# Forgetting attention with 66-row score matmuls: the cumulative gate sums ride in two more rows of the query and key tiles

## The chip, the cores and the metric

The kernel runs as one program on one core of a Trainium2 chip. The metric is the device time of one execution in microseconds (us), and the times shown are medians of several runs. The core's engines run side by side, each through its own list of instructions, and wait for each other on semaphores: TensorE (PE in the profile; its weight loads are a row of their own, PEld), VectorE (DVE), ScalarE (ACT), GpSimd (POOL) and SyncE (SP), which here issues nearly all DMA transfers.

## The reference

Two layers of a decoder trunk on 512 positions of 1024 channels. Each layer is a half-step SwiGLU feed-forward, a mixer with four gated branches, and a second feed-forward. The branches are a Conformer convolution, a short gated convolution, a sliding-window attention, and the forgetting attention ("fox") that this change touches:

```
def _forgetting_attention(q, k, v, log_f):        # 4 heads of 64
    cum = jnp.cumsum(log_f, axis=1)
    ...
        s = jnp.einsum("bqhd,bkhd->bhqk", q_blk, k, ...) * (dh ** -0.5)
        s = s + (c_blk[..., :, None] - cum_k[:, :, None, :])
        s = jnp.where(kpos[None, :] <= qpos[:, None], s, NEG_INF)
        p = jax.nn.softmax(s, axis=-1)
        return jnp.einsum("bhqk,bkhd->bqhd", p.astype(v.dtype), v)
```

`q` and `k` are RMS-normalised over their 64 channels and scaled by a per-channel weight; `log_f` is the log-sigmoid of a gate plus a bias, one per head and position. So a score is a 64-long dot product plus the query position's cumulative gate sum minus the key position's.

## The kernel before, in words

Activations are kept transposed: channels on the 128 partitions, 512 positions along the row. Every float32 product is made of three fp32r matmuls on a high and a low part of each operand (`mm3`, L227 to L230: high by high, low by high, high by low). ScalarE rounds a tile to its high part and VectorE subtracts to get the low part (`split`, L232). Weights stream in from HBM in 512 KB chunks through the SP queue (`load_one`, L185).

The big projections accumulate in four PSUM banks with the tag `mm`; everything else ("background" work of attention and norms) uses the other four banks, tag `bg`. Background work is written as Python generators. `tick()` (L121) is called between two pieces of projection work and moves each active generator one step on, so that attention matmuls stand between projection matmuls. From what is thus written, a scheduler makes the final order on each engine: an instruction may move past others when its inputs or its buffer are not ready by the scheduler's own reckoning. Buffers named `L0`, `L1`, ... (`LT`, L99) exist once; a new tile under the same name has to wait until all reads of the old one are over.

In the mixer, the projection `F` (group F, L646) makes the fox queries and keys, with positions on the partitions, in four `mm` banks. `qk_norm` (L456) copies them to `L0` to `L3`, computes the norm factors, multiplies, and then, one 128-column tile per tick, transposes them with four 128x128 TensorE transposes (L480) into a `bg` bank and splits that into high and low (L483 on ScalarE, L136 on VectorE). Two heads of 64 share the 128 partitions of one tile, so that there are two query tiles and two key tiles.

`forget` (L490) computes `log_f` and its cumulative sums: a tile `lg` with 32 columns per head, of which four are filled, is multiplied in plain float32 with a triangle of ones (L513, four matmuls of 512, 384, 256 and 128 columns). The result has the sums on partitions 32h to 32h+3 for head h. From it, VectorE makes `bq` and `bk`, four rows per head: high and low part of the sum on one side, ones on the other.

`fox_unit(h, i)` (L527) makes the scores of head h and query block i, 256 to 512 columns wide, in one `bg` bank with five matmuls: high by high with 64 rows (L534), the causal mask as a bf16 matmul with the identity, 128 rows (L535), the two cross terms with 64 rows (L536, L537), and `bq` by `bk` with 4 rows (L538). Softmax follows on VectorE and ScalarE, then a transpose of the probabilities (L554) and the product with the values (L569 to L571). There are 4 heads x 4 blocks = 16 units in a layer. Of the four widths of a head, two are 256, one is 384 and one is 512.

After group F, `branch` (L728) runs 8 output tiles for each of the four branches; for tile d a gate projection (24 matmuls into one `mm` bank), six branch matmuls into another, a tanh on ScalarE (L739) and a multiply on VectorE that frees the second bank. In the first branch that multiply writes its result to `L0` to `L7` (`mg_[d]`), where `L0` to `L3` held the untransposed fox queries and keys.

Of the kernel before, what the change touches and what calls it, by code (L numbers as in the profile page):

```python
# [67 lines left out]
def _trunk(tc, xin, wst, wa, wv, wf, par, relb, cst, out):  # L68
# [66 lines left out]
    def stt(o, i0, s, i1, a, b):  # L135
        return V.scalar_tensor_tensor(out=o, in0=i0, scalar=s, in1=i1, op0=a, op1=b)  # L136
# [13 lines left out]
    ones = ct[:, C_ONE:C_ONE + P]  # L150
    one = ct[:, C_1:C_1 + 1]
    ident = ct[:, C_ID:C_ID + P]
    tri = ct[:, C_TRI:C_TRI + S]

    def cm(i):
        return ct[:, C_M + i:C_M + i + 1]

    def pc(l, o, n=1):
        return pt_[:, l * NPAR + o:l * NPAR + o + n]
# [238 lines left out]
    def mixer(l, st, nxt):  # L398
# [54 lines left out]
                confT.append((hi, lo))  # L453
                yield

        def qk_norm(pv, zs, nq, n, offs, res, done):  # L456


            v = T([P, NB, n], F32, f"v{n}")
            for j in range(NB):  # L460
                sq = TP()
                A.copy(zs[j][:, 0:64 * n], pv[j][:, 0:64 * n])
                A.activation(sq[:, 0:64 * n], pv[j][:, 0:64 * n], AF.Square)
                V.tensor_reduce(v[:, j, :], sq[:, 0:64 * n].rearrange("p (h c) -> p h c", c=64), AX.X, ALU.add)
            ts(v[:, :, 0:nq], v[:, :, 0:nq], 1.0, 64 * EPS, ALU.mult, ALU.add)
            ts(v[:, :, nq:n], v[:, :, nq:n], 1.0 / 64, EPS, ALU.mult, ALU.add)
            r = rsq(v.rearrange("p j h -> p (j h)"), NB * n)
            for j in range(NB):
                z = zs[j][:, 0:64 * n].rearrange("p (h c) -> p h c", c=64)
                rj = r[:, j * n:(j + 1) * n].rearrange("p (h o) -> p h o", o=1).to_broadcast([P, n, 64])  # L470
                V.tensor_mul(z, z, rj)
            yield
            yield
            yield
            yield
            for t in range(n // 2):
                yield
                ps = PSB()
                for j in range(NB):
                    nc.tensor.transpose(ps[:, j * P:(j + 1) * P], zs[j][:, t * P:(t + 1) * P], ident)  # L480
                g = pc(l, offs[t])
                hi, lo = LT(res + 2 * t), LT(res + 2 * t + 1)
                A.activation(hi, ps, AF.Identity, scale=g)  # L483
                stt(lo, ps, g, f(hi), ALU.mult, ALU.subtract)
                done.append((hi, lo))


        bq, bk = T([P, S], F32R, "bq"), T([P, S], F32R, "bk")

        def forget():  # L490
            z = fl.rearrange("p j h -> p (j h)")
            ab, e, w, t = SM(16), SM(16), SM(16), SM(16)
            ts(ab, z, -1.0, None, ALU.mult)
            V.tensor_tensor(out=ab, in0=ab, in1=z, op=ALU.min)
            A.activation(e, ab, AF.Exp)
            ts(w, e, 1.0, None, ALU.add)
            A.activation(t, w, AF.Ln)
            stt(e, w, -1.0, e, ALU.add, ALU.subtract)
            V.reciprocal(w, w)
            V.tensor_mul(e, e, w)  # L500
            V.tensor_sub(t, t, e)
            stt(t, z, 0.0, t, ALU.min, ALU.subtract)
            lg = T([P, NB, 4, 32], F32, "L25")
            V.memset(lg, 0.0)
            t3 = t.rearrange("p (j h o) -> p j h o", j=NB, o=1)
            for c in range(4):
                ts(lg[:, :, :, c:c + 1], t3, 1.0 if c < 2 else -1.0, None, ALU.mult)
            yield
            yield
            yield  # L510
            ps = PSB()
            for j in range(NB):
                mm(ps[:, j * P:], lhsT=lg[:, j].rearrange("p h c -> p (h c)"), rhs=tri[:, 0:S - j * P],  # L513
                   start=j == 0, stop=j == NB - 1)
            hi, lo = LT(24), TP()
            A.copy(hi, ps)
            V.tensor_sub(lo, ps, f(hi))
            for o, m in ((bq, 0), (bk, 3)):
                t = TP()
                ts(t, lo, cm(m + 1), cm(m + 2), ALU.mult, ALU.add)  # L520
                stt(o, f(hi), cm(m), t, ALU.mult, ALU.add)


        fo = [(None, None), (None, None)]
        ptile = {}

        def fox_unit(h, i):  # L527
                t, r = h // 2, slice(64 * (h % 2), 64 * (h % 2) + 64)
                W = (i + 1) * P
                N = max(W, 256)  # L530
                qs_, hb = slice(i * P, (i + 1) * P), slice(32 * h, 32 * h + 4)
                ps = PSB()
                (qh, ql), (kh, kl) = qf[t], qf[2 + t]
                mm(ps[:, 0:N], lhsT=qh[r, qs_], rhs=kh[r, 0:N], start=True, stop=False)  # L534
                mm(ps[:, qs_], lhsT=idb, rhs=cmb, start=False, stop=False)  # L535
                mm(ps[:, 0:N], lhsT=qh[r, qs_], rhs=kl[r, 0:N], start=False, stop=False)  # L536
# [294 lines left out]
def _arrays(i):  # L831
# [11 lines left out]
    par = []  # L843
    rep = lambda a: np.broadcast_to(a[None], (P, a.shape[0]))
    col = lambda a: np.tile(a, 2)[:, None]
    for l in range(2):
        w = i["w_in"][l]
        ffn(l, 1)
# [25 lines left out]
        par += [col(i[n][l]) for n in ("swa_q_norm", "swa_k_norm", "fox_q_norm", "fox_k_norm")]  # L874
# [30 lines left out]
```

## Time and profile before

| | |
|---|---|
| median of 3 runs | 2335.91 us (2335.43 to 2338.44) |
| the profiled execution's own time | 2336.04 us |
| its span, first to last instruction | 2334.0 us |
| TensorE busy | 2322.5 us, 10467 matmuls |
| VectorE busy | 1181.5 us |
| ScalarE busy | 797.5 us |
| DMA | 217.57 MB, mean 93 GB/s |
| mean granted TensorE clock | 0.998 of full |

A share of busy time is an average over the whole run. Matmul records have modelled ends and overlap their neighbours: a matmul is shown with 0.39 us although the next starts 0.23 us after it. What a matmul costs in a stream is therefore read from the start of one to the start of the next, in the timeline.

### The profile page before, as it was taken

The page shows a single profiled execution, that of the slowest core. Times are in us where ns is not written, and L with a number is a line of the kernel's source. Part 1 is how long each engine was busy: PE and PEld are TensorE (multiplying, and loading weights), DVE is VectorE, ACT ScalarE, POOL GpSimd, SP SyncE. Part 2 cuts the span into 40 slices and gives each one's busy share as a digit, 9 for nine tenths or more (in the row PEclk, how much of TensorE's full clock was granted, in tenths as well). Part 3 has the DMA queues.
Part 4 walks back from the last instruction along what each step waited for, and adds up shares of the span by engine and source line. Part 5 has one row for each costly group of instructions (what it writes and reads, how often), then busy time and mean ns, then how long its engine had stood idle before and what let it go on. Part 6 is the DMA issues. An engine that isn't in the chain of part 4 may idle for free.

```text
span 2334.0 us, 25909 instructions
## 1 busy us (share of the span) xinstructions
PE 2322.5 (100%) x10467; PEld 1907.3 (82%) x10467; DVE 1181.5 (51%) x1770; ACT 797.5 (34%) x1176; POOL 3.8 (0%) x9
## 2 busy tenths in 40 slices
PE   9999999999999999999999999999999999999999
PEld 6788888887788888888888888888877888888887
DVE  5433446675664554344454334467656645443442
ACT  4322334554433332222232222345543333322221
POOL 0000000000000000000000000000000000000000
PEclk9999999999999999999999999999999999999999
DMA  5433332322223333333323333322222232333332
GB/s 146 123 100 96 94 100 82 100 73 73 62 83 97 94 98 100 94 96 99 99 91 100 96 94 100 100 88 85 73 73 63 83 98 91 109 94 96 99 99 91
DMA packets 62120, 217.57 MB, mean 93 GB/s; under 512 B 7408, under 2 KB 7540, under 8 KB 62000
## 3 DMA queue, kind: packets, MB, share of 16 engines
q1 hardware_dynamic: 61056, 214.54, 29.5%
q0 software_dynamic: 944, 1.37, 0.4%
q8 instruction: 82, 1.34, 0.2%
q14 instruction: 38, 0.31, 0.0%
HBM read 213.00 MB, written 2.88 MB: 92 GB/s over the span
## 4 chain that ended last, share of the span: by engine, by line
PE 98%; DMA 2%; ACT 0%; DVE 0%; issue 0%; SPq 0%; ACTq 0%; DVEq 0%
PE mm L228 31%; PE mm L230 31%; PE mm L229 31%; DMA ws<-wst 1%; PE bg L534 0%; PE bg L536 0%; PE bg L538 0%; PE bg L554 0%; PE bg L252 0%; PE bg L480 0%; PE bg L615 0%; DMA x<-xin 0%; PE bg L570 0%; PE bg L535 0%; PE bg L537 0%; PE bg L571 0%
## 5 line engine op out<-in xcount | busy, mean ns | idle before, releaser
L233 ACT CAST wh<-ws 128x1024 fp32r<-128x1024 f32 (+1 forms) x406 | 421.5, 1039 | 1207.1 <-PE mm L229 923.4
L228 PE MATMUL mm<-xh,wh 128*128 128x512 f32 x2080 | 815.7, 393 | 3.1 <-ACT wh L233 2.8
L230 PE MATMUL mm<-xh,wl 128*128 128x512 f32 x2080 | 812.8, 391 | 1.5 <-DVE wl L234 1.5
L229 PE MATMUL mm<-xl,wh 128*128 128x512 f32 x2080 | 811.7, 391 | 0.7 <-DVE xl L136 0.6
L234 DVE TENSOR_TENSOR wl<-ws,wh 128x1024 fp32r<-128x1024 f32 (+1 forms) x406 | 489.6, 1207 | 550.1 <-ACT wh L233 544.6
L228 PEld LDWEIGHTS mm<-xh,wh 128*128 128x128 f32 x2080 | 391.0, 188 | 90.1 <-ACT wh L233 4.5
L230 PEld LDWEIGHTS mm<-xh,wl 128*128 128x128 f32 x2080 | 391.3, 188 | 87.2 <-DVE wl L234 5.9
L229 PEld LDWEIGHTS mm<-xl,wh 128*128 128x128 f32 x2080 | 391.3, 188 | 83.0 <-DVE xl L136 1.5
L228 PE MATMUL mm<-L,wh 128*128 128x512 f32 x960 | 373.7, 389 | 1.3 <-ACT tp L739 1.3
L230 PE MATMUL mm<-L,wl 128*128 128x512 f32 x960 | 373.6, 389 | 0.0
L229 PE MATMUL mm<-L,wh 128*128 128x512 f32 x960 | 373.4, 389 | 0.0
L228 PEld LDWEIGHTS mm<-L,wh 128*128 128x128 f32 x960 | 180.2, 188 | 39.1 <-ACT tp L739 1.8
L230 PEld LDWEIGHTS mm<-L,wl 128*128 128x128 f32 x960 | 180.2, 188 | 37.4
L229 PEld LDWEIGHTS mm<-L,wh 128*128 128x128 f32 x960 | 180.2, 188 | 37.3
L338 DVE TENSOR_TENSOR tp<-mm,L 128x512 f32<-128x512 f32 x88 | 60.8, 691 | 267.7 <-PE mm L230 267.7
L336 DVE TENSOR_TENSOR tp<-mm,L 128x512 f32<-128x512 f32 x88 | 60.8, 691 | 182.8 <-PE mm L230 182.8
L136 DVE SCALAR_TENSOR_TENSOR cacc<-u,par,cacc 128x512 f32<-128x512 f32 x120 | 89.2, 743 | 31.7 <-PE mm L230 31.4
L233 ACT CAST L<-tp 128x512 fp32r<-128x512 f32 x96 | 59.9, 623 | 56.8 <-DVE tp L339 56.6
L228 PE MATMUL mm<-wh,xh 128*128 128x384 f32 (+2 forms) x192 | 69.3, 361 | 0.0
L229 PE MATMUL mm<-wl,xh 128*128 128x384 f32 (+2 forms) x192 | 68.1, 355 | 0.0
L230 PE MATMUL mm<-wh,xl 128*128 128x384 f32 (+2 forms) x192 | 68.0, 354 | 0.0
L136 DVE SCALAR_TENSOR_TENSOR x<-mm,x 128x512 f32<-128x512 f32 x80 | 54.6, 688 | 24.8 <-PE mm L230 24.2
(169 smaller groups left out, 1268.1 us busy)
## 6 DMA issues: line engine op xcount, KB each, us to landing
ws<-wst SPq DMA_DIRECT2D x378, 512.0 KB, 3.5
ws<-wf SPq DMA_DIRECT2D x8, 512.0 KB, 3.6
ws<-wv SPq DMA_DIRECT2D x8, 388.0 KB, 3.1
ws<-wa SPq DMA_DIRECT2D x8, 384.0 KB, 3.1
x<-xin SPq DMA_DIRECT2D x8, 256.0 KB, 5.9
out<-x SPq DMA_DIRECT2D x8, 256.0 KB, 2.4
ws<-wst SPq DMA_DIRECT2D x4, 256.0 KB, 5.4
toep<-tp POOLq DMA_DIRECT2D x1, 768.0 KB, 33.6
```

The source lines that it names most:

```text
L136: return V.scalar_tensor_tensor(out=o, in0=i0, scalar=s, in1=i1, op0=a, op1=b)
L228: mm(ps, lhsT=w[0], rhs=xx[0], start=first, stop=False)
L229: mm(ps, lhsT=w[0], rhs=xx[1], start=False, stop=False)
L230: unit[0] = mm(ps, lhsT=w[1], rhs=xx[0], start=False, stop=last)
L233: A.copy(o_hi, src)
L234: V.tensor_sub(o_lo, src, f(o_hi))
L336: V.tensor_mul(sg, pg, rb)
L338: V.tensor_mul(us, pu, rb)
```

## The change

The cumulative gate sums become two more channels of every query and key. For each head, the untransposed query tile gets 66 columns instead of 64: its 64 channels, the cumulative sum, and a one; the key tile its 64 channels, a one, and minus the cumulative sum. Their dot product is then score plus sum minus sum, and the fifth matmul of a unit goes, with `bq`, `bk` and the masks that built them. Each head now has tiles of its own that start at partition 0 (66 rows), so that there are eight tiles to transpose instead of four, with four 66-column transposes each, two tiles per tick. Queries stand in `L0` to `L3` before the transpose and keys in `L4` to `L7`; the split tiles take `L8` to `L15` and eight new buffers `L30` to `L37`. `forget` turns its matmul around (the triangle is the stationary operand, the 16 gate columns move) and leaves the sums with positions on the partitions, from where VectorE copies them into the 66-column tiles (eight small copies). The constants shrink from 903 to 641 columns, and the GpSimd queue's scratch space is set to 4096 bytes, which makes room for the new buffers. `qk_a`, the other user of `qk_norm`, is written out and does what it did.

```diff
@@ -48,10 +48,9 @@
 C_ONE = 0
 C_ID = 128
 C_TRI = 256
-C_CM = 768
-C_M = 896
-C_1 = 902
-C_OH = 903
+C_CM = 512
+C_1 = 640
+C_OH = 641
...
@@ -453,39 +449,25 @@
-        def qk_norm(pv, zs, nq, n, offs, res, done):
-
+        def qk_rsq(pv, nq, n):
 
             v = T([P, NB, n], F32, f"v{n}")
             for j in range(NB):
                 sq = TP()
-                A.copy(zs[j][:, 0:64 * n], pv[j][:, 0:64 * n])
                 A.activation(sq[:, 0:64 * n], pv[j][:, 0:64 * n], AF.Square)
...
-            for t in range(n // 2):
-                yield
-                ps = PSB()
-                for j in range(NB):
-                    nc.tensor.transpose(ps[:, j * P:(j + 1) * P], zs[j][:, t * P:(t + 1) * P], ident)
-                g = pc(l, offs[t])
-                hi, lo = LT(res + 2 * t), LT(res + 2 * t + 1)
-                A.activation(hi, ps, AF.Identity, scale=g)
-                stt(lo, ps, g, f(hi), ALU.mult, ALU.subtract)
-                done.append((hi, lo))
-
-
-        bq, bk = T([P, S], F32R, "bq"), T([P, S], F32R, "bk")
+            return r.rearrange("p (j h o) -> p j h o", j=NB, o=1)
+
+        def qk_put(ps, g, hi, lo, done):
+            A.activation(hi, ps, AF.Identity, scale=g)
+            stt(lo, ps, g, f(hi), ALU.mult, ALU.subtract)
+            done.append((hi, lo))
...
@@ -500,43 +482,36 @@
-            lg = T([P, NB, 4, 32], F32, "L25")
-            V.memset(lg, 0.0)
-            t3 = t.rearrange("p (j h o) -> p j h o", j=NB, o=1)
-            for c in range(4):
-                ts(lg[:, :, :, c:c + 1], t3, 1.0 if c < 2 else -1.0, None, ALU.mult)
+
+            cq, ck = T([P, NB, 4, 2], F32, "cq"), T([P, NB, 4, 2], F32, "ck")
+            V.memset(cq, 1.0)
+            V.memset(ck, 1.0)
             yield
             yield
             yield
             ps = PSB()
-            for j in range(NB):
-                mm(ps[:, j * P:], lhsT=lg[:, j].rearrange("p h c -> p (h c)"), rhs=tri[:, 0:S - j * P],
-                   start=j == 0, stop=j == NB - 1)
-            hi, lo = LT(24), TP()
-            A.copy(hi, ps)
-            V.tensor_sub(lo, ps, f(hi))
-            for o, m in ((bq, 0), (bk, 3)):
-                t = TP()
-                ts(t, lo, cm(m + 1), cm(m + 2), ALU.mult, ALU.add)
-                stt(o, f(hi), cm(m), t, ALU.mult, ALU.add)
+            mm(ps[:, 0:16], lhsT=tri[:, 0:P], rhs=t, start=True, stop=False)
+            for j in range(1, NB):
+                mm(ps[:, 4 * j:16], lhsT=tri[:, P:2 * P], rhs=t[:, 0:16 - 4 * j], start=False, stop=j == NB - 1)
+            c = ps[:, 0:16].rearrange("p (j h o) -> p j h o", j=NB, o=1)
+            V.tensor_copy(cq[:, :, :, 0:1], c)
+            ts(ck[:, :, :, 1:2], c, -1.0, None, ALU.mult)
+            cum["q"], cum["k"] = cq, ck
...
         def fox_unit(h, i):
-                t, r = h // 2, slice(64 * (h % 2), 64 * (h % 2) + 64)
                 W = (i + 1) * P
                 N = max(W, 256)
-                qs_, hb = slice(i * P, (i + 1) * P), slice(32 * h, 32 * h + 4)
+                qs_ = slice(i * P, (i + 1) * P)
                 ps = PSB()
-                (qh, ql), (kh, kl) = qf[t], qf[2 + t]
-                mm(ps[:, 0:N], lhsT=qh[r, qs_], rhs=kh[r, 0:N], start=True, stop=False)
+                (qh, ql), (kh, kl) = qf[h], qf[4 + h]
+                mm(ps[:, 0:N], lhsT=qh[:, qs_], rhs=kh[:, 0:N], start=True, stop=False)
                 mm(ps[:, qs_], lhsT=idb, rhs=cmb, start=False, stop=False)
-                mm(ps[:, 0:N], lhsT=qh[r, qs_], rhs=kl[r, 0:N], start=False, stop=False)
-                mm(ps[:, 0:N], lhsT=ql[r, qs_], rhs=kh[r, 0:N], start=False, stop=False)
-                mm(ps[:, 0:N], lhsT=bq[hb, qs_], rhs=bk[hb, 0:N], start=False, stop=True,
-                   tile_position=(32 * h, 0))
+                mm(ps[:, 0:N], lhsT=qh[:, qs_], rhs=kl[:, 0:N], start=False, stop=False)
+                mm(ps[:, 0:N], lhsT=ql[:, qs_], rhs=kh[:, 0:N], start=False, stop=True)
...
         def qk_f(pv):
-            yield from qk_norm(pv, [LT(j, F32) for j in range(NB)], 4, 8, (O_FQ, O_FQ, O_FK, O_FK), 8, qf)
+
+            zs = [[LT(j, F32)[:, 0:264].rearrange("p (h c) -> p h c", c=66),
+                   LT(4 + j, F32)[:, 0:264].rearrange("p (h c) -> p h c", c=66)] for j in range(NB)]
+            for j in range(NB):
+                for s_ in range(2):
+                    A.copy(zs[j][s_][:, :, 0:64], pv[j][:, 256 * s_:256 * s_ + 256].rearrange("p (h c) -> p h c", c=64))
+            r = qk_rsq(pv, 4, 8)
+            for j in range(NB):
+                for s_ in range(2):
+                    z = zs[j][s_][:, :, 0:64]
+                    V.tensor_mul(z, z, r[:, j, 4 * s_:4 * s_ + 4].to_broadcast([P, 4, 64]))
+            for _ in range(4):
+                yield
+            for j in range(NB):
+                V.tensor_copy(zs[j][0][:, :, 64:66], cum["q"][:, j])
+                V.tensor_copy(zs[j][1][:, :, 64:66], cum["k"][:, j])
+            for t in range(8):
+                if t % 2 == 0:
+                    yield
+                ps = PSB()
+                for j in range(NB):
+                    nc.tensor.transpose(ps[0:66, j * P:(j + 1) * P], zs[j][t // 4][:, t % 4, :], ident)
+                b = 8 + 2 * t if t < 4 else 22 + 2 * t
+                qk_put(ps[0:66, :], pc(l, (O_FQ, O_FK)[t // 4])[0:66], LT(b)[0:66, :], LT(b + 1)[0:66, :], qf)
...
@@ -890,7 +903,8 @@
-    nc = _bacc.Bacc("TRN2", target_bir_lowering=False, num_devices=1)
+    nc = _bacc.Bacc("TRN2", target_bir_lowering=False, num_devices=1,
+                    dynamic_dma_scratch_size=4096)
```

What is left out are the same cuts in the constants, `qk_a`, and the host code that lays out the constants and norm weights (the fox norm weights are followed by ones instead of being repeated).

TensorE, the first two score units of head 0 in the first layer (`bg` is the unit's bank, `L_...` are the query and key parts, `cmb` and `idb` the mask and the identity, `mm` the next gate projection). Before:

```order
L534 MATMUL bg_4115<-L_714_4052,L_688_3900 128x256
L535 LDWEIGHTS idb_75
L535 MATMUL bg_4115<-cmb_76,idb_75 128x128
L536 MATMUL bg_4115<-L_715_4053,L_688_3900 128x256
L537 MATMUL bg_4115<-L_714_4052,L_689_3901 128x256
L538 MATMUL bg_4115<-bk_2555,bq_2554 128x256
L534 MATMUL bg_4128<-L_714_4052,L_688_3900 128x256
L535 LDWEIGHTS idb_75
L535 MATMUL bg_4128<-cmb_76,idb_75 128x128
L536 MATMUL bg_4128<-L_715_4053,L_688_3900 128x256
L537 MATMUL bg_4128<-L_714_4052,L_689_3901 128x256
L538 MATMUL bg_4128<-bk_2555,bq_2554 128x256
```

The same place now (lines L511 to L514 are the four matmuls that are left):

```order
L511 MATMUL bg_4159<-L_719_4078,L_687_3908 128x256
L512 LDWEIGHTS idb_75
L512 MATMUL bg_4159<-cmb_76,idb_75 128x128
L513 MATMUL bg_4159<-L_720_4079,L_687_3908 128x256
L514 MATMUL bg_4159<-L_719_4078,L_688_3909 128x256
L511 MATMUL bg_4171<-L_719_4078,L_687_3908 128x256
L512 LDWEIGHTS idb_75
L512 MATMUL bg_4171<-cmb_76,idb_75 128x128
L513 MATMUL bg_4171<-L_720_4079,L_687_3908 128x256
L514 MATMUL bg_4171<-L_719_4078,L_688_3909 128x256
```

One matmul per unit is gone; the order of the others is the same. The shapes printed are those of the result and do not show the rows: 64, 128, 64, 64 and 4 before, 66, 128, 66 and 66 now. The built program gives the 64-row matmuls a tile of 64x128 of the array, the 4-row ones a tile of 32x128, and the 128-row and 66-row ones the whole 128x128.

TensorE, tile d = 2 of the first branch in the first layer, where the gate projection into `mm_4011` ends and the branch matmuls into `mm_4012` begin. Before:

```order
L230 MATMUL mm_4011<-xh_477_2731,wl_3855 128x512
L480 MATMUL bg_4047<-cst_73,L_615_3537 128x128
L480 MATMUL bg_4047<-cst_73,L_616_3538 128x128
L480 MATMUL bg_4047<-cst_73,L_617_3539 128x128
L480 MATMUL bg_4047<-cst_73,L_618_3540 128x128
L480 MATMUL bg_4106<-cst_73,L_615_3537 128x128
L480 MATMUL bg_4106<-cst_73,L_616_3538 128x128
L480 MATMUL bg_4106<-cst_73,L_617_3539 128x128
L480 MATMUL bg_4106<-cst_73,L_618_3540 128x128
L228 MATMUL mm_4012<-L_528_3049,wh_3610 128x512
```

The same place now, where the projection is `mm_4037` and the branch matmuls go into `mm_4038`:

```order
L226 MATMUL mm_4037<-xh_475_2729,wl_3863 128x512
L224 MATMUL mm_4038<-L_526_3047,wh_3610 128x512
L225 MATMUL mm_4038<-L_527_3048,wh_3610 128x512
L226 MATMUL mm_4038<-L_526_3047,wl_3611 128x512
L224 MATMUL mm_4038<-L_651_3734,wh_3610 128x512
L225 MATMUL mm_4038<-L_652_3735,wh_3610 128x512
L226 MATMUL mm_4038<-L_651_3734,wl_3611 128x512
L689 MATMUL bg_4073<-cst_73,L_611_3526 66x128
```

The last reads of `L0` to `L3` stood ahead of the branch matmuls of d = 2. Now these are query tiles, which are read for the last time one tick earlier; the transposes that follow here read the key tiles in `L4` to `L7`.

VectorE, the same stretch: the three multiplies that write `mg_[0]` to `mg_[2]` into `L0` to `L2` and free the second bank of tiles 0, 1 and 2. Before:

```order
L234 TENSOR_TENSOR L_703_3972<-bg_3988,L_702_3971 64x512
L136 SCALAR_TENSOR_TENSOR L_672_3818<-tp_3816,mm_3785 128x512
L136 SCALAR_TENSOR_TENSOR L_686_3893<-tp_3891,mm_3860 128x512
L136 SCALAR_TENSOR_TENSOR L_697_3953<-tp_3951,mm_3920 128x512
L234 TENSOR_TENSOR wl_4007<-ws_4005,wh_4006 128x1024
```

And now:

```order
L230 TENSOR_TENSOR wl_3932<-ws_3930,wh_3931 128x1024
L135 SCALAR_TENSOR_TENSOR L_671_3818<-tp_3816,mm_3785 128x512
L135 SCALAR_TENSOR_TENSOR L_685_3901<-tp_3899,mm_3868 128x512
L135 SCALAR_TENSOR_TENSOR L_699_3970<-tp_3968,mm_3937 128x512
L135 SCALAR_TENSOR_TENSOR L_702_3978<-bg_3972,par_72,L_701_3977 66x512
```

They moved up: before, they stood behind the splits of the sliding-window output (`L_703`), now they stand ahead of the split of the third query tile (`L_702`).

## Rows read from the trace of the kernel before

**Rows 1.** The page: busy time by engine, and the chain that ended last.
```profile
PE 2322.5 (100%) x10467; PEld 1907.3 (82%) x10467; DVE 1181.5 (51%) x1770; ACT 797.5 (34%) x1176; POOL 3.8 (0%) x9
...
PE 98%; DMA 2%; ACT 0%; DVE 0%; issue 0%; SPq 0%; ACTq 0%; DVEq 0%
```

**Rows 2.** Who waited for whom, TensorE, whole run: total us, times, longest.
```profile
PE mm L228 <- ACT tp L739: 1.3, 2, 0.7
```

**Rows 3.** Timeline of TensorE, two 256-column units: start us, us, engine, line, operands, count.
```profile
538.71 0.39 PE L228 MATMUL mm<-xh,wh 128*128 128x512 f32 x1
...
543.01 0.39 PE L230 MATMUL mm<-L,wl 128*128 128x512 f32 x1
543.33 0.38 PE L534 MATMUL bg<-L,L 64*128 64x256 f32 x1
543.65 0.23 PE L535 MATMUL bg<-cmb,idb 128*128 128x128 bf16 x1
543.81 0.38 PE L536 MATMUL bg<-L,L 64*128 64x256 f32 x1
544.03 0.28 PE L537 MATMUL bg<-L,L 64*128 64x256 f32 x1
544.24 0.38 PE L538 MATMUL bg<-bk,bq 4*128 4x256 f32 x1
544.54 0.38 PE L534 MATMUL bg<-L,L 64*128 64x256 f32 x1
...
545.75 0.50 PE L228 MATMUL mm<-xh,wh 128*128 128x512 f32 x1
546.10 0.39 PE L229 MATMUL mm<-xl,wh 128*128 128x512 f32 x1
```

**Rows 4.** Timeline of TensorE, 256-column matmuls of 128 rows behind one another.
```profile
525.11 0.28 PE L634 MATMUL bg<-pth,vh 128*128 128x256 f32 x1
525.23 0.28 PE L635 MATMUL bg<-ptl,vh 128*128 128x256 f32 x1
```

**Rows 5.** Timeline of the weight loads around the first of them.
```profile
542.79 0.19 PEld L230 LDWEIGHTS mm<-L,wl 128*128 128x128 f32 x1
543.33 0.18 PEld L534 LDWEIGHTS bg<-L,L 64*128 64x128 f32 x1 [0.35 <-issue]
```

**Rows 6.** Timeline of TensorE, a 384-column and a 512-column unit.
```profile
552.68 0.49 PE L554 MATMUL bg<-cst,sp 128*128 128x128 f32 x3
...
553.91 0.34 PE L537 MATMUL bg<-L,L 64*128 64x384 f32 x1
554.18 0.43 PE L538 MATMUL bg<-bk,bq 4*128 4x384 f32 x1
...
556.54 0.39 PE L229 MATMUL mm<-xl,wh 128*128 128x512 f32 x1
```

**Rows 7.** Timeline at tile d = 2 of the first branch, TensorE and VectorE.
```profile
533.25 1.03 PE L480 MATMUL bg<-cst,L 128*128 128x128 f32 x8
...
534.00 1.88 DVE L136 SCALAR_TENSOR_TENSOR L<-tp,mm 128x512 f32<-128x512 f32 x3 [3.54 <-PE bg L480]
...
534.94 0.50 PE L228 MATMUL mm<-L,wh 128*128 128x512 f32 x1 [0.65 <-ACT tp L739]
```

**Rows 8.** Busy time by window: PE, PEld, DVE, ACT, POOL, granted clock, DMA.
```profile
609.50:612.95 3.45, 3.45 (x10) 2.67 (x9) 1.77 (x5) 2.00 (x4) 0.00 (x0) 0.51 0.02 5
```

**Rows 9.** Timeline of TensorE, the cumulative sums and what follows them.
```profile
463.32 2.32 PE L513 MATMUL bg<-cst,L 128*128 128x512 f32 x8
465.47 0.38 PE L615 MATMUL bg<-cst,sp 128*128 128x128 f32 x2
```

**Rows 10.** Timeline of TensorE, float32 matmuls of one column.
```profile
19.43 0.95 PE L252 MATMUL bg<-cst,L 128*128 128x1 f32 x8
20.24 0.48 PE L229 MATMUL mm<-xl,wh 128*128 128x512 f32 x1
```

**Rows 11.** Groups of instructions, splits behind the transposes: busy us, mean ns, idle before.
```profile
L483 ACT ACTIVATE L<-bg,par 128x512 fp32r<-128x512 f32 x14 | 9.4, 687 | 1.2 <-PE bg L480 1.2
```

More of the change, by code (lines that the diff above doesn't have):

```diff
@@ L152, in _trunk @@
     ident = ct[:, C_ID:C_ID + P]
-    tri = ct[:, C_TRI:C_TRI + S]
-    def cm(i):
-        return ct[:, C_M + i:C_M + i + 1]
+    tri = ct[:, C_TRI:C_TRI + 2 * P]
     def pc(l, o, n=1):
@@ L467, in qk_norm @@
             r = rsq(v.rearrange("p j h -> p (j h)"), NB * n)
-            for j in range(NB):
-                z = zs[j][:, 0:64 * n].rearrange("p (h c) -> p h c", c=64)
-                rj = r[:, j * n:(j + 1) * n].rearrange("p (h o) -> p h o", o=1).to_broadcast([P, n, 64])
-                V.tensor_mul(z, z, rj)
-            yield
-            yield
-            yield
-            yield
-            for t in range(n // 2):
-                yield
-                ps = PSB()
-                for j in range(NB):
-                    nc.tensor.transpose(ps[:, j * P:(j + 1) * P], zs[j][:, t * P:(t + 1) * P], ident)
-                g = pc(l, offs[t])
-                hi, lo = LT(res + 2 * t), LT(res + 2 * t + 1)
-                A.activation(hi, ps, AF.Identity, scale=g)
-                stt(lo, ps, g, f(hi), ALU.mult, ALU.subtract)
-                done.append((hi, lo))
-        bq, bk = T([P, S], F32R, "bq"), T([P, S], F32R, "bk")
+            return r.rearrange("p (j h o) -> p j h o", j=NB, o=1)
[3 more added lines that the diff above has]
+            done.append((hi, lo))
+        cum = {}
         def forget():
@@ L511, in forget @@
             ps = PSB()
-            for j in range(NB):
-                mm(ps[:, j * P:], lhsT=lg[:, j].rearrange("p h c -> p (h c)"), rhs=tri[:, 0:S - j * P],
-                   start=j == 0, stop=j == NB - 1)
-            hi, lo = LT(24), TP()
-            A.copy(hi, ps)
-            V.tensor_sub(lo, ps, f(hi))
-            for o, m in ((bq, 0), (bk, 3)):
-                t = TP()
-                ts(t, lo, cm(m + 1), cm(m + 2), ALU.mult, ALU.add)
-                stt(o, f(hi), cm(m), t, ALU.mult, ALU.add)
+            mm(ps[:, 0:16], lhsT=tri[:, 0:P], rhs=t, start=True, stop=False)
[5 more added lines that the diff above has]
+            cum["q"], cum["k"] = cq, ck
         fo = [(None, None), (None, None)]
@@ L670, in qk_a @@
         def qk_a(pv):
-            yield from qk_norm(pv, [LT(4 + j, F32) for j in range(NB)], 4, 6, (O_AQ, O_AQ, O_AK), 16, qa)
+            zs = [LT(4 + j, F32) for j in range(NB)]
+            for j in range(NB):
+                A.copy(zs[j][:, 0:384], pv[j][:, 0:384])
+            r = qk_rsq(pv, 4, 6)
+            for j in range(NB):
+                z = zs[j][:, 0:384].rearrange("p (h c) -> p h c", c=64)
+                V.tensor_mul(z, z, r[:, j].to_broadcast([P, 6, 64]))
+            for _ in range(4):
+                yield
+            for t, o in enumerate((O_AQ, O_AQ, O_AK)):
+                yield
+                ps = PSB()
+                for j in range(NB):
+                    nc.tensor.transpose(ps[:, j * P:(j + 1) * P], zs[j][:, t * P:(t + 1) * P], ident)
+                qk_put(ps, pc(l, o), LT(16 + 2 * t), LT(17 + 2 * t), qa)
             for pr in range(2):
@@ L676, in qk_f @@
         def qk_f(pv):
-            yield from qk_norm(pv, [LT(j, F32) for j in range(NB)], 4, 8, (O_FQ, O_FQ, O_FK, O_FK), 8, qf)
+            zs = [[LT(j, F32)[:, 0:264].rearrange("p (h c) -> p h c", c=66),
[4 more added lines that the diff above has]
+            r = qk_rsq(pv, 4, 8)
+            for j in range(NB):
+                for s_ in range(2):
+                    z = zs[j][s_][:, :, 0:64]
+                    V.tensor_mul(z, z, r[:, j, 4 * s_:4 * s_ + 4].to_broadcast([P, 4, 64]))
+            for _ in range(4):
+                yield
+            for j in range(NB):
+                V.tensor_copy(zs[j][0][:, :, 64:66], cum["q"][:, j])
+                V.tensor_copy(zs[j][1][:, :, 64:66], cum["k"][:, j])
+            for t in range(8):
+                if t % 2 == 0:
+                    yield
+                ps = PSB()
+                for j in range(NB):
+                    nc.tensor.transpose(ps[0:66, j * P:(j + 1) * P], zs[j][t // 4][:, t % 4, :], ident)
+                b = 8 + 2 * t if t < 4 else 22 + 2 * t
+                qk_put(ps[0:66, :], pc(l, (O_FQ, O_FK)[t // 4])[0:66], LT(b)[0:66, :], LT(b + 1)[0:66, :], qf)
             for h in range(4):
@@ L804, in _constants @@
     c[:, C_TRI:C_TRI + P] = p[:, None] <= p[None]
-    c[:, C_TRI + P:C_TRI + S] = 1.0
+    c[:, C_TRI + P:C_TRI + 2 * P] = 1.0
     c[:, C_CM:C_CM + P] = np.where(p[None] <= p[:, None], 0.0, NEG)
-    r = p % 32
-    for i, m in enumerate((r == 0, r == 1, (r == 2) | (r == 3), r == 2, r == 3, (r == 0) | (r == 1))):
-        c[:, C_M + i] = m
     c[:, C_1] = 1.0
@@ L845, in _arrays @@
     col = lambda a: np.tile(a, 2)[:, None]
+    one = lambda a: np.concatenate([a, np.ones_like(a)])[:, None]
     for l in range(2):
@@ L873, in _arrays @@
         par += [i["sc_conv"][l][:, c * P:(c + 1) * P].T for c in range(2)]
-        par += [col(i[n][l]) for n in ("swa_q_norm", "swa_k_norm", "fox_q_norm", "fox_k_norm")]
+        par += [col(i[n][l]) for n in ("swa_q_norm", "swa_k_norm")]
+        par += [one(i[n][l]) for n in ("fox_q_norm", "fox_k_norm")]
         par += [rep(i["swa_sink"][l][[0, 2, 1, 3]]), rep(i["b_forget"][l])]
```

## The prediction

> **What bounds the kernel.** I read the page first. TensorE is busy for all of the span, and the chain of work that ended last runs over it for 98% [rows 1]. VectorE and ScalarE are busy for half and a third. So work taken from or given to TensorE counts in full, and work on other engines only where TensorE waits for it. The list of waits is the second view: apart from the first 80 us of the program, TensorE waits in one kind of place, twice 0.65 us in front of branch matmuls [rows 2]. The third view is the timeline of TensorE, read from start to start. Nineteen steps between projection matmuls of 512 columns, from 538.71 to 543.01, take 4.30 us, 0.226 each. Then come two score units of 256 columns, and nothing of theirs keeps that pace [rows 3]: L534 begins 0.32 us after the matmul ahead of it, the mask 0.32 after L534, L536 0.16 after the mask, L537 0.22 later, L538 0.21 later, and the next unit 0.30 after that. A 256-column matmul of 128 rows among its like takes 0.12 [rows 4]. The fourth view says why. The load of weights for the projection matmul of 543.01 begins at 542.79, beside the matmul ahead of it; the load for L534 begins at 543.33, with L534 itself, after 0.35 us without any load [rows 5]. In a score unit the tile of the array changes from 64 rows to 128, to 64, to 4, and at each change a load of 0.18 us stands bare.
>
> The Trainium skill, page "TensorEngine Tiling (Array Packing)", section Available Configurations, lists row tiles of 128, 64 and 32 rows and none between; section Key Properties says that a change of tiling mode drains the engine. By the two, 66 rows run as a full array, and the term for the scores is the whole one below. No matmul of 66 rows is in the trace of before to show it.
>
> **The scores.** From 543.01 to 546.10 are 3.09 us; two ordinary steps in it are 0.45, so two 256-column units cost 2.64 with the way in and out [rows 3]. For a 384- and a 512-column unit: 552.68 to 556.54 is 3.86 [rows 6]; in it are three transposes and one ordinary step. Eight transposes are shown with 1.03 and three with 0.49 [rows 6, 7], so one adds 0.108. That leaves 3.86 - 0.33 - 0.23 = 3.30. One head is 5.94, and 4 heads x 2 layers 47.5 us. The 16 units of a layer stand in 11 runs instead of the 8 counted so; each further run has a way in (0.32 - 0.23) and a way out (546.10 - 545.75 - 0.23), 0.21 together, and six of them 1.3. Before: 48.8 us.
>
> After, if 66 rows run as 128 do, nothing changes the tile. The matmuls of a unit then cost 0.12, 0.17 (between the neighbours) or 0.23 by width [rows 3, 4], three each. For the mask I take 0.11, what a transpose with as many weight columns costs; its bounds are 0.05, half of a 256-column matmul, and 0.16, what it takes now. Units: 0.47, 0.62, 0.80; a head 2.36; eight 18.9. **Scores: -29.9 us** (-31.8 to -28.3 by the mask alone). The other bound is that the loads stay bare; it is a rival below.
>
> **The granted clock.** It fell to half (1.2 instead of 2.4 GHz) for one stretch in each layer's fox part: 0.51 from 609.50 to 612.95 [rows 8], and again in the second layer. It followed directly on a 384- and a 512-column unit, in which loads stood bare. In 3.45 us, 49% were lost: 1.7 us, two times 3.3 to 3.4. With these units at full pace I expect neither. **-3.3 us**, bounds 0 and -3.4.
>
> **The cumulative sums.** L513 has two passes of four float32 matmuls, 2.15 us to the next instruction [rows 9]. The new ones move 16 to 4 columns; eight passes of one column take 20.24 - 19.43 = 0.81 [rows 10]. -1.34 twice: **-2.7 us**. The VectorE work on 512 columns behind them (tp, bq, bk) becomes small copies; VectorE is off the path there, so I count nothing.
>
> **The transposes.** 32 instead of 16 per layer, over both layers 64 for 32. The old ones cost 32 x 0.108 = 3.5 us. The new ones load 66 columns of weights instead of 128 and move the same 128. If the load sets the price, as the one-column matmul suggests (0.10 with nothing to move) [rows 10], one costs half, 0.055: +0.0. If the moved columns do, 0.108: +3.5. I take 0.07, nearer to the load: **+1.0 us**. Each transposed tile has a split on ScalarE of 0.69 us [rows 11] and a like one on VectorE; there are four more per layer. They lie beside projections of 24 x 0.226 = 5.4 us per tick, which cover two of each. If that cover were gone, a tick would wait for one pair more, about 0.7 us, in four ticks per layer: 5.5 us.
>
> **The wait at tile d = 2.** Before, the eight transposes end about 534.12 and the branch matmul starts at 534.94 [rows 7]. VectorE had waited 3.54 us for these transposes, because its three multiplies write `L0` to `L2`, which they were the last to read; only then could it free the second bank of the earlier tiles. In the new order the last query transposes stand one tick earlier and the branch matmuls follow the projection directly. So 0.82 goes, and with it the slow first step behind it, 0.11; twice **-1.9 us**. Next in line is ScalarE's tanh, which ended about then as well [rows 2]; if it holds TensorE as long, the term is 0.
>
> **Other edits at nothing.** The constants' load is 134 KB shorter and lies behind the first weights in SP's queue; the start may shift by 1 us either way. The eight sum copies, the smaller ScalarE copies of group F (eight of 256 for four of 512) and the new buffers run on engines with idle time; bank by bank, the copies of F still stand between the squares, so each `mm` bank is free as early. The order of POOL and SP is otherwise as before. The smaller scratch leaves POOL's instructions the same.
>
> **Sum.** -29.9 - 3.3 - 2.7 + 1.0 - 1.9 = -36.8. The profiled execution took 2336.04 us, 0.13 above the median; 2336.04 - 36.8 - 0.13 gives 2299.1. I forecast **2299 us**.
>
> **Rivals.**
> Clock and wait stay: the two half-clock stretches only move, and the tanh holds TensorE as the multiplies did. Then 2299.1 + 3.3 + 1.9 = 2304.3. For it: both depend on what stands around, not on the scores alone. Against: what preceded the clock's fall is gone. Chance 0.14.
>
> 66 rows change the tile like 64 did. Then the mask (128 rows) still splits each unit, and only the fifth matmul goes: L537's 0.21 to 0.27 (the closing step of 0.30 stays), 0.21 twice, 0.27 and 0.32 per head [rows 3, 6], 1.0, eight times 8.1. With sums, transposes and wait, -8.1 - 2.7 + 1.0 - 1.9 = -11.7: 2324.2. For it: no matmul of an odd row count is in the trace. Against: the program gives the 66-row matmuls the same tile as the projections. Chance 0.08.
>
> Each load stands bare in front of its matmul, though the tile stays. For it: L537 follows L536 in the same tile and still takes 0.22, not 0.12 [rows 3]. 96 matmuls x 0.18 [rows 5] = 17.3: 2316.4. Against: in the stream of projections the loads begin beside the matmul ahead. Chance 0.04. The Trainium skill has a rule that would make it so, in "TensorE: Matmul & The Clock Gate", section The mechanism: a load overlaps a running matmul only when its row group differs. By that rule all 66-row loads would be bare; [rows 5] disagree with it for 128 rows.
>
> Slower: the clock. If the denser stretch of transposes, four to eight at a time between short matmuls, made the half clock last, each 3.45 us of it would cost 1.7. The gain without the clock term is 33.5 us; from 20 stretches on over both layers the kernel is slower. With 30 it would be 2302.4 + 30 x 1.7 = 2353. For it: both falls lie in this part. Against: there were two in 2334 us, and the clock is full at the eight transposes of before. Chance 0.03.
>
> **How the numbers follow.** The forecast has 0.69, the rivals 0.14, 0.08, 0.04 and 0.03; 0.02 is left for no change. The measurement tells 0.2%, 4.7 us, from no change. All cases but the last two are faster by more: faster 0.95, same 0.02, slower 0.03. The forecast alone reaches from 2294 (a cheap mask, free transposes, a lucky start) to 2307 (dear transposes, the wait, 2 to 3 us of splits). The range goes on into the first rival and its costs: 2293 to 2312.
>
> **What would show it.** In the new timeline the four matmuls of a 256-column unit step by 0.12, 0.11, 0.12, 0.12, with loads beside the matmul ahead; steps of 0.2 to 0.3 mean that a rival on the loads is right. No window of the fox part at half clock. Waits on L739's successor gone. The new transposes step by 0.055 to 0.11. TensorE's list grows by no matmul in all: 32 transposes come, 32 score matmuls go. The prediction is wrong if TensorE shows a new wait of over 2 us per layer around group F or the fox units.

## The result, and the profile after

The changed kernel took 2302.98 us (median), the kernel before, run beside it, 2337.16: a ratio of 0.9853, 95% interval 0.9834 to 0.9873. One disturbed run, 7589.9 us at a mean clock of 0.338, counts in this median (2302.64 without it) but not in the ratio. The profiled execution took 2302.64, 33.4 us less than that of before; the forecast was 36.8 less, 2299 us.

The page after [rows 1], busy time by engine:

```profile
PE 2290.1 (100%) x10467; PEld 1898.5 (83%) x10467; DVE 1182.5 (51%) x1790; ACT 801.0 (35%) x1190; POOL 3.8 (0%) x9
```

TensorE has as many matmuls as before and is busy 32.4 us less; it still bounds the kernel. The two 256-column units of head 0 in the new timeline of TensorE [rows 3]:

```profile
542.00 1.04 PE L689 MATMUL bg<-cst,L 128*66 128x128 f32 x8
542.79 0.36 PE L511 MATMUL bg<-L,L 66*128 66x256 f32 x1
543.00 0.23 PE L512 MATMUL bg<-cmb,idb 128*128 128x128 bf16 x1
...
543.36 0.29 PE L511 MATMUL bg<-L,L 66*128 66x256 f32 x1
543.49 0.23 PE L512 MATMUL bg<-cmb,idb 128*128 128x128 bf16 x1
543.52 0.37 PE L513 MATMUL bg<-L,L 66*128 66x256 f32 x1
543.73 0.28 PE L514 MATMUL bg<-L,L 66*128 66x256 f32 x1
543.85 0.40 PE L224 MATMUL mm<-xh,wh 128*128 128x512 f32 x1
544.08 0.40 PE L225 MATMUL mm<-xl,wh 128*128 128x512 f32 x1
```

From the second L511 to L224 is 0.49 us for a whole unit, where the forecast had 0.47; the projection behind it keeps its pace at once. The single steps in it are 0.13, 0.03, 0.21 and 0.12: the mask's record starts late and the next one follows it closely, so that only their sum, 0.24, can be held against the forecast's 0.11 and 0.12. The first L511 looks longer (0.21), but the eighth transpose ahead of it is shorter for it: eight take 0.79, not 8 x 0.109. The weight loads in the same stretch [rows 5]:

```profile
543.00 0.20 PEld L513 LDWEIGHTS bg<-L,L 66*128 66x128 f32 x1
543.12 0.19 PEld L514 LDWEIGHTS bg<-L,L 66*128 66x128 f32 x1
543.24 0.19 PEld L511 LDWEIGHTS bg<-L,L 66*128 66x128 f32 x1
```

The loads for L513 (543.04), L514 (543.24) and the next L511 (543.36) now begin 0.04 to 0.12 us ahead of their matmuls, beside the one before; the pause of 0.35 us without a load is gone.

Before, half the clock was granted behind the unit whose last matmul starts at 608.36 [rows 8]. The same matmul starts at 597.41 in the new profile, and the window around it (the seventh value behind the times is the clock) is:

```profile
595.40:610.00 14.60, 14.60 (x74) 12.07 (x73) 12.15 (x22) 7.97 (x18) 0.00 (x0) 1.00 0.24 73
```

No window of 25 us over the whole run shows less than 0.99.

The cumulative sums [rows 9], and the tile of the first branch in which TensorE had waited [rows 7], with VectorE's multiplies:

```profile
463.27 0.29 PE L493 MATMUL bg<-sm,cst 128*128 128x16 f32 x2
463.41 0.81 PE L495 MATMUL bg<-sm,cst 128*128 128x12 f32 x6
464.08 0.41 PE L590 MATMUL bg<-cst,sp 128*128 128x128 f32 x2
...
532.71 0.39 PE L226 MATMUL mm<-xh,wl 128*128 128x512 f32 x1
532.93 0.39 PE L224 MATMUL mm<-L,wh 128*128 128x512 f32 x1
```

```profile
523.91 1.88 DVE L135 SCALAR_TENSOR_TENSOR L<-tp,mm 128x512 f32<-128x512 f32 x3
```

The sums take 0.81 us in place of 2.15. The branch matmul of 532.93 follows the projection at the ordinary step; the three multiplies run 10 us earlier than before, and the list of waits holds none from 80 to 2280 us, so the four more splits per layer have stayed under cover.

### The profile page after: what moved, and what is told of

It is laid out like the page before. It is cut to its first block, busy times and chain, and to the rows that moved or that the text cites. A ratio compares the mean times of both kernels' runs of the same rounds, so it can differ in the third digit from the quotient of the medians.

```text
span 2300.6 us, 25938 instructions
## 1 busy us (share of the span) xinstructions
PE 2290.1 (100%) x10467; PEld 1898.5 (83%) x10467; DVE 1182.5 (51%) x1790; ACT 801.0 (35%) x1190; POOL 3.8 (0%) x9
## 4 chain that ended last, share of the span: by engine, by line
PE 98%; DMA 2%; ACT 0%; DVE 0%; issue 0%; SPq 0%; ACTq 0%; DVEq 0%
PE mm L224 31%; PE mm L226 31%; PE mm L225 31%; DMA ws<-wst 1%; PE bg L529 0%; PE bg L689 0%; PE bg L513 0%; PE bg L248 0%; PE bg L590 0%; DMA x<-xin 0%; PE bg L545 0%; PE bg L511 0%; PE bg L546 0%; PE bg L544 0%; PE bg L514 0%; PE bg L224 0%
## 5 line engine op out<-in xcount | busy, mean ns | idle before, releaser
L224 PE MATMUL mm<-xh,wh 128*128 128x512 f32 x2080 | 812.8, 392 | 3.4 <-ACT wh L229 3.4
L225 PE MATMUL mm<-xl,wh 128*128 128x512 f32 x2080 | 810.2, 390 | 0.7 <-DVE xl L135 0.6
L224 PEld LDWEIGHTS mm<-xh,wh 128*128 128x128 f32 x2080 | 390.4, 188 | 86.7 <-ACT wh L229 5.4
L225 PEld LDWEIGHTS mm<-xl,wh 128*128 128x128 f32 x2080 | 390.7, 188 | 82.3 <-DVE xl L135 1.5
L224 PE MATMUL mm<-L,wh 128*128 128x512 f32 x960 | 373.5, 389 | 0.0
L225 PE MATMUL mm<-L,wh 128*128 128x512 f32 x960 | 373.5, 389 | 0.0
L224 PEld LDWEIGHTS mm<-L,wh 128*128 128x128 f32 x960 | 180.2, 188 | 37.4
L225 PEld LDWEIGHTS mm<-L,wh 128*128 128x128 f32 x960 | 180.2, 188 | 37.3
L224 PE MATMUL mm<-wh,xh 128*128 128x384 f32 (+2 forms) x192 | 69.3, 361 | 0.0
L225 PE MATMUL mm<-wl,xh 128*128 128x384 f32 (+2 forms) x192 | 68.1, 355 | 0.0
```

Source lines behind the costliest of these rows:

```text
L224: mm(ps, lhsT=w[0], rhs=xx[0], start=first, stop=False)
L225: mm(ps, lhsT=w[0], rhs=xx[1], start=False, stop=False)
```

## The experiments

To compare kernels, the score steps were summed: for each of the 22 runs of units, from the start of the matmul ahead of it to the start of the second one behind it, less the ordinary steps of those two (0.227 us for 512 columns, 0.12 for 256, 0.109 for a transpose). Before this is 48.9 us over both layers, after 19.9. Two explanations were set against each other: the changes of the array's tile, or simply the removed fifth matmul. Differences to the changed kernel are taken from 2302.98 us; measured again below it took 2302.48, so they are good to about half a microsecond. The kernel before took 2335.97 to 2336.67 beside the experiments.

**64 rows again.** The changed kernel, scores over the first 64 rows only.

```diff
-                mm(ps[:, 0:N], lhsT=qh[:, qs_], rhs=kh[:, 0:N], start=True, stop=False)
+                c = slice(0, 64)
+                mm(ps[:, 0:N], lhsT=qh[c, qs_], rhs=kh[c, 0:N], start=True, stop=False)
...
```

> The changed kernel with its three score matmuls cut to the first 64 rows, so that the gate sums are left out of the scores; the mask keeps its 128 rows, the order and all columns stay. Theory (the gain is that no unit changes the tile of the array): the changes come back, a unit costs about 1.0 us with 256 columns, 1.17 with 384 and 1.35 with 512 and 0.21 more per run of units, so that the scores cost about 40.8 us instead of 19.2: 2324 us, up to 2328 if the half-clock stretches return; L511 to L513 step by 0.2 to 0.32. Rival (the gain is the fifth matmul that went): no step changes, 2303 us.

2317.93 us, +15.0 (ratio to before 0.9922, 0.9907 to 0.9936). Its timeline of TensorE:

```profile
542.66 0.38 PE L512 MATMUL bg<-L,L 64*128 64x256 f32 x1
542.98 0.23 PE L513 MATMUL bg<-cmb,idb 128*128 128x128 bf16 x1
543.14 0.38 PE L514 MATMUL bg<-L,L 64*128 64x256 f32 x1
543.36 0.28 PE L515 MATMUL bg<-L,L 64*128 64x256 f32 x1
543.48 0.28 PE L512 MATMUL bg<-L,L 64*128 64x256 f32 x1
```

Same matmuls, same columns, and 0.82 us from L512 to L512. So a changed tile costs. But from the last 64-row matmul to the first of the next unit, which stay in one tile, is only 0.12, and the theory had priced that step as a change, too. Score steps 35.0: 15.0 more than after.

**Before without its fifth matmul.**

```diff
-                mm(ps[:, 0:N], lhsT=ql[r, qs_], rhs=kh[r, 0:N], start=False, stop=False)
-                mm(ps[:, 0:N], lhsT=bq[hb, qs_], rhs=bk[hb, 0:N], start=False, stop=True,
-                   tile_position=(32 * h, 0))
+                mm(ps[:, 0:N], lhsT=ql[r, qs_], rhs=kh[r, 0:N], start=False, stop=True)
```

> The kernel before without its fifth matmul of 4 rows (the gate sums are left out of the scores; they are still computed). Theory: the 64-row and 128-row tiles still change in each unit, so only the fifth's own 0.21 to 0.32 goes, 1.0 us per head, 8.1 in all: 2328 to 2329 us. Rival (the fifth matmul was the price): most of the 30 us go, about 2307 us.

2319.26 us, 16.7 less than before (0.9927, 0.9910 to 0.9944): twice what the theory said, half of what the rival said. Score steps 35.0, 13.8 less; the other 3 us agree with the clock, which is full here. TensorE's timeline, and the window around the unit that stood ahead of the half clock before, whose last matmul starts at 603.35 here:

```profile
544.18 0.28 PE L537 MATMUL bg<-L,L 64*128 64x256 f32 x1
544.30 0.27 PE L534 MATMUL bg<-L,L 64*128 64x256 f32 x1
544.50 0.23 PE L535 MATMUL bg<-cmb,idb 128*128 128x128 bf16 x1
```

```profile
600.00:609.50 9.50, 9.50 (x43) 7.08 (x42) 6.32 (x12) 4.82 (x11) 0.00 (x0) 1.00 0.18 57
```

L537 to the next L534 is 0.12 here, and 0.51 before, across the fifth matmul [rows 3: 544.03 to 544.54]. The theory had taken off that matmul's own step and left the change on its far side.

**A fifth matmul that keeps the tile.** The changed kernel with low part by low part added.

```diff
-                mm(ps[:, 0:N], lhsT=ql[:, qs_], rhs=kh[:, 0:N], start=False, stop=True)
+                mm(ps[:, 0:N], lhsT=ql[:, qs_], rhs=kh[:, 0:N], start=False, stop=False)
+                mm(ps[:, 0:N], lhsT=ql[:, qs_], rhs=kl[:, 0:N], start=False, stop=True)
```

> The changed kernel with a fifth matmul of 66 rows per unit again, low part by low part, nothing left out. Theory: in an unchanged tile it costs its columns, 0.12 us with 256, 0.17 with 384 and 0.23 with 512: 16 x 0.12 + 8 x 0.17 + 8 x 0.23 = 5.1 us in 32 units, 2308 us. Rival (a fifth matmul costs what it cost before, 0.31 to 0.42 with what it did to the next step): 11.3 us, 2314 us.

2308.12 us (0.9879, 0.9864 to 0.9893), +5.1; score steps +5.1. TensorE's timeline, the end of a unit of 256 columns:

```profile
544.33 0.28 PE L515 MATMUL bg<-L,L 66*128 66x256 f32 x1
544.45 0.40 PE L224 MATMUL mm<-xh,wh 128*128 128x512 f32 x1
```

In an unchanged tile a fifth matmul costs its columns and no more.

**64 rows without a change inside a run.** The first experiment without the mask matmul.

> The changed kernel with score matmuls of 64 rows and without the mask matmul (gate sums and mask are left out of the scores), so that inside a run of units every matmul has the same tile of 64 rows. Theory (the price is paid at a change of the tile only): the steps inside a run are 0.12, 0.17 and 0.23 us by width, and each of the 22 runs pays one change in and one out, 0.21 us together: 4.6 us, less the 32 mask matmuls at 0.11: 3.5 us; 2302.6 + 4.6 - 3.5, about 2304 us. Rival (a load of 64 rows stands bare in front of every matmul, changed tile or not): 96 steps longer by 0.10, about 2312 us.

2307.56 us (0.9874, 0.9857 to 0.9890), between the two. TensorE's timeline:

```profile
543.38 0.38 PE L512 MATMUL bg<-L,L 64*128 64x256 f32 x1
543.60 0.28 PE L513 MATMUL bg<-L,L 64*128 64x256 f32 x1
543.72 0.28 PE L514 MATMUL bg<-L,L 64*128 64x256 f32 x1
543.84 0.28 PE L512 MATMUL bg<-L,L 64*128 64x256 f32 x1
543.96 0.28 PE L513 MATMUL bg<-L,L 64*128 64x256 f32 x1
544.08 0.28 PE L514 MATMUL bg<-L,L 64*128 64x256 f32 x1
544.28 0.50 PE L224 MATMUL mm<-xh,wh 128*128 128x512 f32 x1
```

Between changes the 64-row matmuls step by 0.12 like any others, so the rival (bare loads for 64 rows) is out. The two ends of a run are dearer than the 0.21 assumed: against the same three matmuls with 66 rows (the kernel with VectorE's mask, below, which has 32 adds on VectorE besides) this kernel takes 8.7 us more, 0.40 for each of the 22 runs, or about 0.20 for each of their 44 ends.

**Keys first.** The tiles transposed in the other order.

```diff
-                (qh, ql), (kh, kl) = qf[h], qf[4 + h]
+                (qh, ql), (kh, kl) = qf[4 + h], qf[h]
...
-            for t in range(8):
+            for t in (4, 5, 6, 7, 0, 1, 2, 3):
```

> The changed kernel with the key tiles transposed ahead of the query tiles, so that the buffers of mg_[0] to mg_[3] are read for the last time later; nothing left out. Theory (the wait at d = 2 was the multiplies' wait for the query transposes): TensorE waits again in front of the branch matmuls of d = 2 or d = 3, 0.8 us or more per layer, 2304.5 us or more, and VectorE's multiplies wait for PE bg L689. Rival (the wait was ScalarE's tanh or went with the order): no wait after 80 us, 2303 us.

2303.95 us (0.9862, 0.9847 to 0.9877), +1.0. The wait is back, smaller. TensorE, ScalarE and VectorE there:

```profile
532.78 1.47 PE L689 MATMUL bg<-cst,L 128*66 128x128 f32 x12
534.46 0.50 PE L224 MATMUL mm<-L,wh 128*128 128x512 f32 x1 [0.21 <-ACT tp L753]
```

```profile
532.74 1.04 ACT L229 CAST wh<-ws 128x1024 fp32r<-128x1024 f32 x1 [3.29 <-PE mm L225]
533.81 0.60 ACT L753 ACTIVATE tp<-mm 128x512 f32<-128x512 f32 x1
```

```profile
536.40 2.47 DVE L135 SCALAR_TENSOR_TENSOR L<-tp,mm 128x512 f32<-128x512 f32 x4
```

The multiplies run two microseconds after TensorE went on, so they did not release it. ScalarE's tanh ends at 534.41 and TensorE starts at 534.46, and before, too, it was ScalarE that released this matmul [rows 7]. The account that fits is this: with three banks held by the late multiplies, the branch matmuls must take the bank of their own gate, which the tanh frees. That the banks are shared out so is read from the program; no row shows it. The tanh ends 1.63 us after TensorE turns from the gate to the transposes (532.78 to 534.41), because ScalarE has a weight cast of 1.04 us in hand until 533.78. Twelve transposes at 0.109 fill 1.31 of that and leave, with 0.05 to the start, 0.37; before, eight filled 0.87 and left 0.82 [rows 7]. Theory and rival were both half right: the wait comes back with the late multiplies, the tanh sets how long it is.

**Short transposes.** Four of 66 by 66 ahead of each four.

```diff
+                for j in range(NB):
+                    nc.tensor.transpose(ps[0:66, j * P:j * P + 66], zs[j][t // 4][0:66, t % 4, :], ident[0:66, 0:66])
```

> The changed kernel with four further transposes ahead of each four, 66 by 66 instead of 128 by 66, whose results are overwritten; nothing left out. If the moved columns set what a transpose costs, a short one steps by 0.056 us, 64 of them 3.6 us: about 2306 us. If a fixed price per load and matmul does, 0.109, 64 of them 7.0 us: about 2310 us.

2306.34 us (0.9869, 0.9855 to 0.9884), +3.4. TensorE:

```profile
515.13 0.40 PE L689 MATMUL bg<-cst,L 66*66 66x66 f32 x4
515.36 0.60 PE L691 MATMUL bg<-cst,L 128*66 128x128 f32 x4
515.80 0.40 PE L689 MATMUL bg<-cst,L 66*66 66x66 f32 x4
```

Four short ones take 0.23, 0.057 each; four with 128 moved columns 0.44, 0.109. The weight columns are 66 in both, and the records of the loads are 0.112 us in both, so the load does not set the price of the longer ones. The rows differ as well as the moved columns (66 and 128); no run parts these two.

**The mask on VectorE.** The mask matmul goes, and VectorE adds the mask in the bank.

```diff
-                mm(ps[:, qs_], lhsT=idb, rhs=cmb, start=False, stop=False)
...
+                V.tensor_add(ps[:, qs_], ps[:, qs_], ct[:, C_CM:C_CM + P])
```

> The changed kernel with the causal mask added by VectorE on the 128 columns of the diagonal block in the bank, instead of by the bf16 matmul; nothing left out. If the mask matmul costs TensorE its 0.11 us and VectorE's 32 adds of about 0.25 us stay off the path: 32 x 0.11 = 3.5 us less, about 2299 us. Rival (the adds delay the softmax, and a unit's transposes or banks hold TensorE): no gain or a loss, 2303 us or more.

2298.83 us (0.9836, 0.9822 to 0.9851). Beside the changed kernel on one chip:

> VectorE's mask once more, beside the changed kernel on one chip. If the difference of 4 us is real, about 2299 us and 3 to 4 us below the changed kernel; if it was the chip, the two agree within 1 us.

> The changed kernel once more, unchanged, beside the two others: about 2303 us.

2298.85 against 2302.48 us: 3.6 less, which is 0.11 for each of the 32 mask matmuls, as the prediction had taken for them. The adds are 32 of 0.286 us, and no wait of TensorE appears:

```profile
L514 DVE TENSOR_TENSOR bg<-bg,cst 128x128 f32<-128x128 f32 x32 | 8.1, 286 | 0.0
```

**Full rows in the sliding window.** The same cure for the other 64-row scores of the kernel, in the kernel with VectorE's mask.

```diff
+                    kh, kl = qa[2 + hf]
...
-                    mm3(ps[:, 0:256], (qh[r, qs_], ql[r, qs_]), (kh[r, c0:c0 + 256], kl[r, c0:c0 + 256]),
+                    mm3(ps[:, 0:256], (qh[:, qs_], ql[:, qs_]), (kh[:, c0:c0 + 256], kl[:, c0:c0 + 256]),
...
+                    for i, b in ((0, 20), (1, 30)):
+                        g = SM(1)
+                        ts(g, pc(l, o), half[:, i:i + 1], None, ALU.mult)
+                        qk_put(ps, g, LT(b), LT(b + 1), qa)
```

> The kernel with VectorE's mask, and in it the 64-row score matmuls of the sliding-window attention, 16 times three per layer, made 128 rows: the key tile is split twice, with the other head's 64 rows scaled to zero; nothing left out. Theory (a change of the tile costs about 0.2 us wherever it is): in the changed kernel the sliding window has 9 runs of 64-row matmuls per layer, each with steps 0.38 to 0.40 us over those of an unchanged tile; 18 x 0.39 = 7.0 us go: about 2292 us. Rival (the price was particular to the forgetting attention, or the two further splits hold TensorE): 2298 us or more.

2298.57 us (0.9837, 0.9824 to 0.9850), against 2298.85 with 64 rows beside it: the 7 us did not come. In the changed kernel, with 64 rows:

```profile
464.08 0.41 PE L590 MATMUL bg<-cst,sp 128*128 128x128 f32 x2
464.43 0.39 PE L224 MATMUL bg<-L,L 64*128 64x256 f32 x2
464.65 0.29 PE L225 MATMUL bg<-L,L 64*128 64x256 f32 x2
464.77 0.28 PE L226 MATMUL bg<-L,L 64*128 64x256 f32 x2
464.98 0.50 PE L224 MATMUL mm<-wh,xh 128*128 128x512 f32 x1
465.32 0.40 PE L225 MATMUL mm<-wl,xh 128*128 128x512 f32 x1
```

And with 128 rows:

```profile
464.34 0.41 PE L593 MATMUL bg<-cst,sp 128*128 128x128 f32 x2
464.51 0.36 PE L224 MATMUL bg<-L,L 128*128 128x256 f32 x1
464.71 0.28 PE L225 MATMUL bg<-L,L 128*128 128x256 f32 x1
...
465.19 0.28 PE L226 MATMUL bg<-L,L 128*128 128x256 f32 x1
465.31 0.40 PE L224 MATMUL mm<-wh,xh 128*128 128x512 f32 x1
465.54 0.40 PE L225 MATMUL mm<-wl,xh 128*128 128x512 f32 x1
```

The changes went: L224 to L225 at the end is 0.23 instead of 0.34. But with 64 rows two matmuls, on the upper and the lower half of the array, run side by side: the two of an "x2" start 0.01 us apart, and the middle pair (L225) takes the 0.12 us of one; the pairs at the two changes take 0.22 and 0.21. Full rows give this up and step three times more, 0.36 us, for the 0.39 that was to go. From the transposes to the second projection matmul are 1.24 us with 64 rows and 1.20 with 128. My estimate had added up the long steps and left out the ones that were shorter than usual. The Trainium skill, "TensorEngine Tiling (Array Packing)", section Theoretical Speedup, gives up to 2x for 64 rows; the trace agrees for the middle pair (0.12 us for two, as for one).

## Why the prediction was right

The time was held, and four of its five terms came out.

- **Scores**, -29.9 forecast, -28.9 measured by the steps: before 48.9 for the 48.8 counted, after 19.9 for the 18.9 forecast. By the experiments it is made of three parts: the fifth matmul's columns, 5.1 (what one costs in an unchanged tile); the changes it brought, 13.8 - 5.1 = 8.7, 42 changes of 0.21; and the remaining 108 changes between 64 and 128 rows, 15.0, at 0.14 in the mean. These are not all alike: at about 0.20 for the 44 ends of runs (8.7, the experiment without the mask), some 6.3 are left for the 64 changes to and from the mask, 0.10 each. Neither explanation alone holds; the fall of the bare loads is shown, and the forecast, which needed only the sum, did not depend on the split. The rival "66 rows change the tile" at 2324 was mispriced by the same mistake: the kernel that does what it describes took 2318.
- **Full array for 66 rows**: the step of 0.12 and the overlapping loads show it. A step of 0.21 is there as well (L513 to L514), which the prediction's own sign would have put to a rival; but the mask's step ahead of it is 0.03, and the four together take 0.49. The picture of a bare load of 0.18 us at each change was too even: the mask's load is 0.10 in both kernels. The rule that loads overlap only when the row group differs (the Trainium skill, "TensorE: Matmul & The Clock Gate", section The mechanism) does not hold here, as it did not before: the load for L514 begins at 543.12 and L513, of the same rows, runs from 543.04.
- **The clock**, -3.3: no half-clock stretch is left in the fox part, as forecast. The reason given is at most a part of it. Units with bare loads stand in both kernels that keep 64 rows with the mask (2318 and 2319 us), and the clock of both is 1.00 from 592 to 618 and from 1740 to 1775 us; by the reason given it should have fallen there, too. Without the fifth matmul it did not fall; why it fell with it is open, and that the term came out is in part luck. A stretch of low clock can still come in the first 80 us, where TensorE waits: the second measurement of the changed kernel shows 0.93 from 50 to 75 us, the first 1.00.
- **The sums**, -2.7: twice 2.15 - 0.81, as worked out.
- **The wait**, -1.9: gone as forecast, and it comes back when the multiplies are late again; but what released TensorE was the tanh, as [rows 2] and [rows 7] had it. The prediction had put the 0.82 us down to the multiplies and the tanh next in line. (Counted by the banks it is the fourth tile, d = 3; the text called it d = 2.)
- **The transposes** are the mis-sized term. "I take 0.07, nearer to the load", +1.0 us; measured 0.109, the same as with 128 weight columns, +3.5, the upper bound. Moving the same 128 columns set the price, not the load. The one-column matmul [rows 10] showed what a load of 128 columns costs when nothing is moved, not that a smaller load would make a matmul shorter.

By their signs: -28.9 - 3.3 - 2.7 + 3.5 - 1.9 = -33.3; the two executions differ by 33.4. The scores, the sums and the transposes are measured after the change; the clock and the wait are what the trace of before shows as lost, and is gone. Of the 3.4 us missed, 2.5 are the transposes and 1.0 the scores.

## What to carry to other kernels

A short matmul is to be priced from the start of its neighbours: where consecutive matmuls use different row tiles of the array, each change cost 0.10 to 0.21 us here, about as much as a 256-column matmul (0.12) or more, and removing one matmul removes the changes on both its sides. Padding or packing the rows to the full array removes them, but two 64-row tiles that run side by side already pay for theirs. Where a load and a stream overlapped, the larger of the two bounds was the price in both places seen here, and not a value between: 0.10 us for the passes of the sums, which move 16 columns at most, and 0.109 for the transposes, which move 128.

## What was not expected of the hardware

Two 64-row matmuls of 256 columns on different halves of the array took 0.12 us together (464.65 to 464.77, two of L225; the first and the last pair took 0.22 and 0.21 with the change of the tile). In the kernel before, the heads of a fox tile also lay on the two halves, but their units stood one after the other and never ran side by side. A float32 transpose of 66 moved columns took 0.057 us and one of 128 took 0.109, with load records of 0.112 in both.
